# Second MLP's third combination made inside the convolution's output projection, with a hand-written order for the blocks around it

## The chip, the cores and the metric

The kernel runs on one core of one Trainium2 chip. A core has TensorE (PE, matrix products, with its weight loads shown as PEld), VectorE (DVE), ScalarE (ACT), GpSimd (POOL) and SyncE (SP, which here only issues DMAs). The metric is the device time of one execution in microseconds (us). The kernel before ran three times, with a median of 1697.54 us (1696.33 to 1698.54).

## What is computed

Two layers are applied to 768 tokens (a sequence of 512 and one of 256, lying side by side as T = 768 columns) of width 1024. Each layer is a token mixer, a squared-ReLU MLP and a gated embedding, each behind an RMS norm. The edit lies between the second layer's mixer and its MLP:

```python
def short_conv(h, w_in, conv_w, w_out):
    b_gate, c_gate, u = jnp.split(h @ w_in, 3, axis=-1)
    z = c_gate * u
    ...                                        # depthwise, width 3, per sequence
    return (b_gate * conv) @ w_out

h = rms_norm(x, norm_mix[i])
x = x + short_conv(h, conv_w_in[j], conv_w[j], conv_w_out[j])   # layer 1
h = rms_norm(x, norm_mlp[i])
x = x + jnp.square(jax.nn.relu(h @ mlp_w_up[i])) @ mlp_w_down[i]
gate = jax.nn.sigmoid(rms_norm(x, norm_ple[i]) @ ple_w_gate[i])
x = x + (p[i] @ ple_w_proj[i]) * gate
```

`w_out` is 1024 x 1024, `mlp_w_up` 1024 x 4096 and `mlp_w_down` 4096 x 1024, all in float32.

## The kernel before, in words

*Layout.* The residual x is held transposed, as eight blocks `x(m)` of 128 partitions by 768 columns; H = 384 is half of the columns. `PAIRED` is the order 0, 4, 1, 5, 2, 6, 3, 7 in which blocks are worked on, so that m and m + 4 follow each other.

*Float32 products.* Every operand is split into a high part, rounded to a matmul format by ACT, and a low part, the rest, subtracted by DVE (`split`, L82 to L84; `Weights7.high` and `low`, L434 and L445). A product is three matmuls per block: high by high, high by low, low by high.

*Two kinds of product.* A plain product runs over all eight blocks for both halves of the columns. The seven-product form (`product7`, L466) takes a pair of weight blocks and two halves of the input as a 2 x 2 matrix and needs seven products instead of eight; for it, weights are summed on DVE (`sums32`, `sums14`, L409 to L415) and inputs are *combined*: for each m below 4 one combination of x(m) and x(m+4). A combination is two copies with the norm's gain on ACT (`copied`, L326), four sums on DVE (`t13`, L345 and L346; `t42`, L350 and L351), two highs on ACT (L355) and two lows on DVE (L361). There are four of them, for blocks (0, 4), (1, 5), (2, 6) and (3, 7).

*The norm.* `norm.block(m, x(m))` writes the high and low parts of a block (`plain_block`, L304 to L310) and adds its square to an accumulator (L195, L196). When all eight are in, the accumulator is split (`acc_parts`: `ah` on ACT, `al` on DVE), a product with ones sums it over the partitions (`ss`, L235), and `rstd_steps` makes the factor rstd: `logs` (v on DVE at L252, then ln, exp and a square on ACT at L254 to L256, ahead of them `table`, which loads ACT's function table unless `ready` is set), `newton` (L260) and `result` (L267). The MLP's products run on blocks that aren't yet multiplied by rstd; it comes in with the squared ReLU (`rectified`, L938; `squared`, L941).

*Output projection.* `project_add` makes eight products `mm` (L129), adds each to x (L830) and calls `norm.block`. After the blocks with i = 1 and 3 it weaves in the combinations (0, 4) and (1, 5). At i = 4 it fetches the MLP's first weight chunk, at i = 6 and 7 it splits it ("direct" holds w11 and w12, "second" w21 and w22).

*The second MLP.* Chunks u = 0 and 1 are plain (`up_plain`, matmuls at L995), all others take the seven-product form (`up`; its first one, u = 2, has its products in the tiles a, b, c and d). Chunk u = 0 uses "direct" for its first 48 matmuls and "second" for its last 48. While it runs, `up_plain` makes `acc_parts`, the table load, the combination (2, 6), the second chunk's splits, the norm's steps and the combination (3, 7); the second chunk's "direct" part is `zhi` and `zlo`. While u = 1 runs, DVE and ACT make the activations of u = 0 and the sums and splits for u = 2. At u = 2, ACT copies the first product (`c`, L1054) before TensorE may add to its tile again.

*Order.* Inside `tc.manual_schedule(engines={ACT, PE, DVE})` these three engines take their instructions in the order of the program text; this holds for the whole MLP. Outside of it, and so in all of `project_add` before, a scheduler orders them. SP's fetches follow the program's order; the raw weights have three buffers (`wraw`), the split ones two each (`whi`, `wlo`), the plain chunk's "direct" part one (`zhi`, `zlo`).

Of the kernel before, what the change touches and what calls it, by code (L numbers as in the profile page):

```python
# [13 lines left out]
AF = mybir.ActivationFunctionType  # L14
ALU = mybir.AluOpType
# [3 lines left out]
P = 128  # L19
D = 1024  # L20
KB = D // P
# [16 lines left out]
H = T // 2  # L38
# [9 lines left out]
def trunk_kernel(ctx: ExitStack, tc: tile.TileContext, a: dict, out: bass.AP):  # L48
    nc = tc.nc
    act, dve, pe = nc.scalar, nc.vector, nc.tensor  # L50
# [65 lines left out]
    def both(name="mm", tag=None):  # L116

        return [t[:, :H] for t in fresh(name, 2, tag)]
# [4 lines left out]
    def group2(ps, terms, first=True, last=True):  # L123

        n = len(terms)
        for i, (wh, wl, xh, xl) in enumerate(terms):
            for j, (w, x) in enumerate(((wh, xh), (wh, xl), (wl, xh))):
                for t, o, e in pieces(ps):
                    pe.matmul(t, lhsT=w, rhs=x[:, o:e], start=first and i == 0 and j == 0, stop=last and i == n - 1 and j == 2)  # L129
# [22 lines left out]
    def big(name, dt=F32):  # L152

        nonlocal turn
        if more is None:
            return tmp.tile([P, T], dt, tag="t", name=name)
        turn += 1
        return tmp.tile([P, T], dt, tag=f"q{turn % 6}", name=name, bufs=1)

    def terms_of(w, xs, col=0):  # L160

        hi, lo = w
        c = slice(col, col + P)
        return [(wh[:, c], wl[:, c], xh, xl) for wh, wl, xh, xl in zip(hi, lo, *xs)]
# [6 lines left out]
    class Norm:  # L171
# [108 lines left out]
    class Norm7(Norm):  # L280
# [17 lines left out]
        def plain_block(self, m, xb):  # L298
            g = gain(self.i, m)
            if m < KB // 2:  # L300
                for j, t in enumerate((self.place(), slot(self.x12.pop(0), "x12"))):
                    src = xb[:, j * H : j * H + H]
                    hi, lo = t[:, :H], t[:, H:]
                    act.activation(hi, src, AF.Copy, scale=g)  # L304
                    dve.scalar_tensor_tensor(lo, src, g, hi.bitcast(F32), ALU.mult, ALU.subtract)
                    self.xs[("x11", "x12")[j]][m] = hi, lo
            else:
                hi, lo = self.place(), self.place()
                act.activation(hi[:], xb, AF.Copy, scale=g)
                dve.scalar_tensor_tensor(lo[:], xb, g, hi[:].bitcast(F32), ALU.mult, ALU.subtract)  # L310
                for j, k in enumerate(("x21", "x22")):
                    self.xs[k][m - KB // 2] = hi[:, j * H : j * H + H], lo[:, j * H : j * H + H]
# [158 lines left out]
    def mixer_attention():  # L471
# [346 lines left out]
    psum = ctx.enter_context(tc.tile_pool(name="ps", bufs=8, space=PSUM))  # L818
# [4 lines left out]
    def x(m, o=0, n=T):  # L823
        return pairs[m // 2][:, m % 2, o : o + n]

    def add(m, ps, src=None):

        src = x(m) if src is None else src
        for t, o, e in pieces(ps):
            dve.tensor_tensor(x(m)[:, o:e], src[:, o:e], t, ALU.add)  # L830


    PAIRED = [m + i for m in range(KB // 2) for i in (0, KB // 2)]

    def project_add(w, src, norm, behind, first):

        for i, m in enumerate(PAIRED):
            ps = both()
            ts = terms_of(first if i == 0 else weight(w[m], KB), src)
            group2(ps, [ts[k] for k in (*PAIRED[:6], *PAIRED[:5:-1])])  # L840
            add(m, ps)
            norm.block(m, x(m))
            behind(i)

    def up_chunk(l, u):
        f = 4 * (u // 2) + u % 2
        return Weights7(a["up"][l, f], a["up"][l, f + 2], plain=u < PLAIN[l])
# [4 lines left out]
    def weave(*chains):  # L852

        for steps in itertools.zip_longest(*chains):
            for step in steps:
                if step:
                    step()

    def first_chunk(l, norm, early):


        w = []

        def behind(i):
            if i == 4:
                w.append(up_chunk(l, 0))
            if i == 6:
                w[0].split("direct")
            if i == 7:
                w[0].split("second")  # L870
            if i % 2 and i // 2 < early:
                weave(norm.combine(i // 2))

        return w, behind

    ET = mybir.EngineType

    def second_inputs(places):

# [45 lines left out]
        weave(norm.combine(1))  # L925
        return parts

    def mlp(l, norm, nxt, w, places, early, product=None):


        xs = norm.xs
        r = parts = None
        todo = list(range(early, KB // 2))
        groups = [{k: {} for k in QS7.values()} for _ in range(NG)]
        pend = []
# [30 lines left out]
        def late(n=1):  # L966

            for _ in range(n):
                if pend:
                    pend.pop(0)()  # L970

        def up_plain(u, w, make, then):

# [14 lines left out]
            for n, (i, ks, sides) in enumerate(order):  # L988
                for k in range(*ks):
                    m, h = PAIRED[k] % (KB // 2), PAIRED[k] // (KB // 2)  # L990
                    c = slice(P * m, P * m + P)
# [172 lines left out]
                        nxt.block(m, x(m))  # L1164

        ups = [(up if u >= PLAIN[l] else up_plain, u) for u in range(2 * NG)]
        jobs = ups[:2]
        for g in range(NG - 1):
            jobs += [ups[2 * g + 2], (down, g, 0), (down, g, 1), ups[2 * g + 3]]
        with tc.manual_schedule(engines={ET.Activation, ET.PE, ET.DVE}):  # L1170
            if product:
                parts = ahead(norm, product, w, places[5:7] + places[12:])
                todo = todo[2:]
            for i, (job, *args) in enumerate(jobs):
# [12 lines left out]
                w = job(*args, w, make, lambda j: weight(a["down"][l, (NG - 1) * (KB // 2) + j], FG))  # L1187
# [117 lines left out]
    def last_ple(norm, full, rest, prs, ys, finals):  # L1305
# [64 lines left out]

        ET = mybir.EngineType
        with tc.manual_schedule(engines={ET.Activation, ET.PE, ET.DVE}):
# [41 lines left out]
        f = (KB, 2 * KB, 0)[kind] + p  # L1414
        return Weights7(a["w_in"][f], a["w_in"][f + KB // 2], plain)

    def mixer_conv(norm, w, v, norm_parts, held, finals, places, outs):
# [11 lines left out]
        pend, after, kept, done = [], [], {}, {}  # L1429
        ys = [None] * KB, [None] * KB  # L1430
# [160 lines left out]
        ET = mybir.EngineType  # L1591
        with tc.manual_schedule(engines={ET.Activation, ET.PE, ET.DVE}):
            for i, (kind, p) in enumerate(jobs):
# [12 lines left out]
        project_add(a["w_out"], ys, *outs, first=w)  # L1606

    class Last(Norm):
        def __init__(self, o, n, acc, rstd):
# [37 lines left out]
    n3 = Norm7(1, "mix1", xs3, aside3, rest[24], spare=dict(zip(("ah", "al", "v"), old[13:])))  # L1647
    wc = ple(n2, n3)

    n4 = Norm7(3, "mlp1", xs1, act1[7:11], act1[11])  # L1650
    w1, behind = first_chunk(1, n4, 2)
    mixer_conv(n3, *wc, held, finals[:], parts, (n4, behind))
    n5 = Norm(5, "ple1", xs1[:16], xs1[16])
    mlp(1, n4, n5, w1[0], act1, 2)
    last_ple(
        n5,
        full=xs1[17:] + act1[:1],
# [2 lines left out]
        ys=act1[8:11],  # L1660
        finals=((act1[11], act1[12]), (act1[13], xs1[16])),
# [79 lines left out]
```

## Time and profile before

| | |
|---|---|
| median of three runs | 1697.54 us |
| profiled execution | 1697.29 us |
| its span, first to last instruction | 1695.6 us |
| mean granted TensorE clock | 0.993 |
| PE busy | 1651.5 us (97%) |
| PEld busy | 1590.6 us (94%) |
| DVE busy | 1414.4 us (83%) |
| ACT busy | 907.3 us (54%) |
| DMA moved | 144.58 MB, mean 85 GB/s |

Times in the rows are microseconds from the start of the span. A row of the timeline has the start, the duration, the engine, the line of the kernel, the operation, the tile written and those read, the shape and the count, and in brackets how long the engine had been idle and what released it. Rows of the same kind that follow each other are merged; the end of a matmul is modelled, so one matmul's duration (0.34) is longer than its distance to the next (0.175). The granted clock is the share of full speed that TensorE was given.

### The profile page before, as it was taken

Reading aid. Unit: us, or ns where it says so; the run is one execution under the profiler, and the core shown is the slowest. Engines: PE = TensorE matmul, PEld = TensorE weight load, DVE = VectorE, ACT = ScalarE, POOL = GpSimd, SP = SyncE. Lnnn points to the kernel's source line nnn. Section 1 sums busy time; section 2 is a strip of 40 time slices with the busy share of each in tenths; the row PEclk is TensorE's granted clock in tenths of the full one; section 3 lists DMA queues with packets and bytes.
Section 4 is the critical chain, followed back from the end, with each engine's and each line's share of the span. In section 5 each row is a group of like instructions: output and inputs, shape, how many; then the busy total and the mean of one; then the engine's idle time right before and its main releaser. Section 6 shows DMA issues by size and latency. Waiting matters only on the chain.

```text
span 1695.6 us, 24086 instructions
## 1 busy us (share of the span) xinstructions
PE 1651.5 (97%) x9410; PEld 1590.6 (94%) x9410; DVE 1414.4 (83%) x2304; ACT 907.3 (54%) x1451; POOL 1.0 (0%) x12
## 2 busy tenths in 40 slices
PE   8999999989999999999999999999999999999996
PEld 7887788989999999999999999999999999999986
DVE  7588888889999989987888787858999999998776
ACT  6467756755455455544654334545445545554544
POOL 0000000000000000000000000000000000000000
PEclk9999999999999999999999999999999999999998
DMA  8653322212122212222312222211122222222222
GB/s 265 192 138 121 116 69 81 88 50 70 69 76 75 73 67 73 74 91 75 100 60 75 75 74 75 75 51 50 66 72 75 75 70 69 74 74 86 81 77 94
DMA packets 47842, 144.58 MB, mean 85 GB/s; under 512 B 6080, under 2 KB 10688, under 8 KB 47728
## 3 DMA queue, kind: packets, MB, share of 16 engines
q1 hardware_dynamic: 45168, 139.89, 25.0%
q10 hardware_dynamic: 2560, 3.15, 0.7%
q8 instruction: 74, 1.21, 0.3%
q14 instruction: 40, 0.33, 0.1%
HBM read 123.10 MB, written 10.48 MB: 79 GB/s over the span
## 4 chain that ended last, share of the span: by engine, by line
PE 59%; DVE 29%; ACT 8%; issue 3%; DMA 0%; DVEq 0%; ACTq 0%; SPq 0%
PE a L466 18%; PE mm L129 9%; PE mm L138 9%; PE b L466 4%; PE B L466 3%; PE C L466 3%; DVE t L361 3%; DVE wlo L445 3%; DVE y L938 3%; PE gate L138 3%; DVE zlo L445 2%; DVE act L394 1%; PE c L466 1%; ACT y L941 1%; PE d L466 1%
## 5 line engine op out<-in xcount | busy, mean ns | idle before, releaser
L434 ACT ACTIVATE whi<-sum 128x1024 fp32r<-128x1024 f32 x67 | 70.5, 1052 | 146.9 <-PE a L466 146.9
L941 ACT ACTIVATE y<-y 128x768 f32<-128x768 f32 x64 | 53.7, 840 | 144.6 <-DVE y L938 144.4
L466 PE MATMUL a<-xs,whi 128*128 128x384 f32 x624 | 122.2, 337 | 4.1 <-ACT whi L434 3.4
L466 PE MATMUL a<-t,zhi 128*128 128x384 f32 x536 | 111.3, 341 | 4.3 <-ACT c L1054 4.3
L466 PEld LDWEIGHTS a<-xs,whi 128*128 128x128 f32 x624 | 110.1, 188 | 4.8 <-ACT whi L434 3.7
L466 PE MATMUL b<-t,zhi 128*128 128x384 f32 x536 | 108.7, 336 | 0.0
L466 PE MATMUL a<-t,whi 128*128 128x384 f32 x536 | 108.7, 336 | 0.0
L466 PEld LDWEIGHTS a<-t,zhi 128*128 128x128 f32 x536 | 96.1, 190 | 5.2 <-ACT c L1054 5.0
L466 PE MATMUL a<-act,whi 128*128 128x384 f32 x448 | 96.5, 337 | 0.0
L466 PEld LDWEIGHTS a<-t,whi 128*128 128x128 f32 x536 | 94.8, 188 | 0.0
L466 PEld LDWEIGHTS b<-t,zhi 128*128 128x128 f32 x536 | 94.7, 188 | 0.0
L445 DVE TENSOR_TENSOR wlo<-wraw,whi 128x1024 fp32r<-128x1024 f32 x72 | 87.6, 1217 | 6.0 <-ACT whi L434 6.0
L445 DVE TENSOR_TENSOR wlo<-sum,whi 128x1024 fp32r<-128x1024 f32 x67 | 81.8, 1221 | 10.2 <-ACT whi L434 10.2
L1110 DVE TENSOR_TENSOR x<-x,a 128x384 f32<-128x384 f32 x112 | 60.7, 552 | 34.0 <-PE a L466 33.6
L434 ACT ACTIVATE zhi<-sum 128x1024 fp32r<-128x1024 f32 x67 | 71.0, 1060 | 22.7 <-DVE sum L410 22.7
L138 PE MATMUL mm<-xs_mix,whi 128*128 128x512 f32 (+1 forms) x320 | 82.8, 342 | 0.0
L434 ACT ACTIVATE whi<-wraw 128x1024 fp32r<-128x1024 f32 x72 | 75.7, 1052 | 11.5 <-PE C L466 6.0
L445 DVE TENSOR_TENSOR zlo<-sum,zhi 128x1024 fp32r<-128x1024 f32 x67 | 81.5, 1217 | 0.0
L466 PEld LDWEIGHTS a<-act,whi 128*128 128x128 f32 x448 | 79.9, 188 | 0.0
L355 ACT ACTIVATE t<-y 128x768 fp32r<-128x768 f32 x56 | 47.1, 841 | 39.8 <-DVE y L346 29.9
L83 ACT ACTIVATE whi<-wraw 128x1024 fp32r<-128x1024 f32 (+2 forms) x49 | 49.9, 1019 | 33.9 <-PE mm L129 14.0
L466 PE MATMUL a<-xs,wlo 128*128 128x384 f32 x312 | 67.2, 337 | 0.3 <-DVE wlo L445 0.2
(317 smaller groups left out, 4485.6 us busy)
## 6 DMA issues: line engine op xcount, KB each, us to landing
wraw<-in_up SPq DMA_DIRECT2D x64, 512.0 KB, 3.5
wraw<-in_down SPq DMA_DIRECT2D x64, 512.0 KB, 3.5
wraw<-in_w_in SPq DMA_DIRECT2D x24, 512.0 KB, 3.4
wraw<-in_gate SPq DMA_DIRECT2D x16, 512.0 KB, 3.4
pj<-pjs SPq DMA_DIRECT2D x16, 384.0 KB, 3.2
wraw<-in_w_q SPq DMA_DIRECT2D x8, 512.0 KB, 5.0
wraw<-in_w_out SPq DMA_DIRECT2D x8, 512.0 KB, 3.5
x_in<-in_x SPq DMA_DIRECT2D x8, 384.0 KB, 6.9
```

The source lines that it names most:

```text
L83: first = act.activation(hi, src, AF.Copy)
L129: pe.matmul(t, lhsT=w, rhs=x[:, o:e], start=first and i == 0 and j == 0, stop=last and i == n - 1 and j == 2)
L138: pe.matmul(ps[:, o:e], lhsT=w, rhs=x[:, o:e], start=i == 0 and j == 0, stop=i == n - 1 and j == 2,)
L355: act.activation(t[0][:], (self.q1, self.q2)[i][:], AF.Copy)
L361: dve.tensor_tensor(lo[:], (self.q1, self.q2)[i][:], hi[:].bitcast(F32), ALU.subtract)
L394: dve.tensor_tensor(lo[:], self.q2[:], hi[:].bitcast(F32), ALU.subtract)
L434: act.activation(hi[:], src, AF.Copy)
L445: dve.tensor_tensor(lo[:], src, hi[:].bitcast(F32), ALU.subtract)
L466: pe.matmul(ps, lhsT=a, rhs=b, start=start and i == 0, stop=i == len(terms) - 1, skip_group_check=True)
L938: dve.scalar_tensor_tensor(t[:, o:e], src, 0.0, r[:, o:e], op, ALU.mult)
L941: act.activation(t[:], t[:], AF.Square)
L1110: dve.tensor_tensor(t[:, o : o + H], t[:, o : o + H], f, op)
```

## The change

1. `project_add` no longer calls a `behind` function. Blocks i = 0 to 4 stay as they were, with the combinations (0, 4) and (1, 5). From the sixth product on (i = 5) a `manual_schedule` region orders ACT, PE and DVE as written: the split of the seventh weight block, block 5, the split of the eighth, the seventh product, the fetch of the first chunk, the copies and the first sums of the combination (2, 6), the eighth product, and then the splits of the first chunk between the parts of block 6 and of the combination; the rest of the combination, the copy of x(3), the fetch of the second chunk; then block 7, with the accumulator's split, the combination (3, 7) and the second chunk's "second" split.
2. The norm is marked `ready`, so its table load is left out.
3. `mlp` gets `begun`, the second chunk and the accumulator's parts. Its first chunk runs in the new `up_begun`, which has no combination: the first 48 plain matmuls, `ss`, `logs`, the second chunk's "direct" split, `newton`, `result`, then the last 48 matmuls and the squared ReLU. The number of combinations still to be made in the MLP is zero (`early` = 4).
4. `first_chunk` goes.

The diff, without the plain matmul loop, which is copied from `up_plain`:

```diff
-    def project_add(w, src, norm, behind, first):
-
-        for i, m in enumerate(PAIRED):
+    def project_add(w, src, norm, first):
+        def product(i, wt):
             ps = both()
-            ts = terms_of(first if i == 0 else weight(w[m], KB), src)
+            ts = terms_of(wt, src)
             group2(ps, [ts[k] for k in (*PAIRED[:6], *PAIRED[:5:-1])])
+            return ps
...
+        for i in range(5):
+            block(i, product(i, first if i == 0 else weights(i)))
+            if i in (1, 3):
+                weave(norm.combine(i // 2))
+        ps = product(5, weights(5))
+        norm.ready = True
+        with tc.manual_schedule(engines={ET.Activation, ET.PE, ET.DVE}):
+            w6 = weights(6)
+            block(5, ps)
+            w7 = weights(7)
+            ps = product(6, w6)
+            c = up_chunk(1, 0)
+            sums = norm.copied(2, 6)
+            sums.t13()
+            sums.t42()
+            ps7 = product(7, w7)
+            c.high("direct")
+            add(PAIRED[6], ps)
+            c.low("direct")
+            norm.plain_block(PAIRED[6], x(PAIRED[6]))
+            c.high("second")
+            norm.square(PAIRED[6], x(PAIRED[6]))
+            c.low("second")
+            sums.high(0)
+            sums.high(1)
+            norm.copied(3)
+            sums.low(0)
+            sums.low(1)
+            v = up_chunk(1, 1)
+            m = KB - 1
+            add(m, ps7)
+            norm.plain_block(m, x(m))
+            sq = big("sq")
+            act.activation(sq[:], x(m), AF.Square)
+            sums = norm.copied(m)
+            dve.tensor_tensor(norm.acc, norm.acc, sq[:], ALU.add)
+            parts = norm.acc_parts()
+            sums.t13()
+            sums.high(0)
+            v.split("second")
+            sums.t42()
+            sums.high(1)
+            sums.low(0)
+            sums.low(1)
+        return c, v, parts
...
+        def up_begun(u, w, make, then):
+            nonlocal r
+            v, parts = begun
+            ps = [both(f"p{i + 1}", "A") for i in range(2)]
+            plain_block(ps[0], 0, w)
+            ss = norm.sum_squares(psum, parts=parts, tag="C")
+            logs, newton, result = norm.rstd_steps(psum, ss)
+            logs()
+            v.split("direct")
+            newton()
+            result()
+            r = norm.r
+            y = [big(f"y{i + 1}") for i in range(2)]
+            for i in range(2):
+                if i:
+                    plain_block(ps[1], 1, w)
+                for o in range(2):
+                    rectified(y[i], ps[i][o], H * o, H * o + H, ALU.max)
+                if i == 0:
+                    squared(y[0])
+            pend.extend(acts_of(u, *y, y[1]))
+            return v
...
-    w1, behind = first_chunk(1, n4, 2)
-    mixer_conv(n3, *wc, held, finals[:], parts, (n4, behind))
+    w1, *begun = mixer_conv(n3, *wc, held, finals[:], parts, n4)
     n5 = Norm(5, "ple1", xs1[:16], xs1[16])
-    mlp(1, n4, n5, w1[0], act1, 2)
+    mlp(1, n4, n5, w1, act1, KB // 2, begun=begun)
```

More of the change, by code (lines that the diff above doesn't have):

```diff
@@ L830, in add, with weights, block @@
             dve.tensor_tensor(x(m)[:, o:e], src[:, o:e], t, ALU.add)
+    ET = mybir.EngineType
     PAIRED = [m + i for m in range(KB // 2) for i in (0, KB // 2)]
-    def project_add(w, src, norm, behind, first):
-        for i, m in enumerate(PAIRED):
+    def project_add(w, src, norm, first):
+        def product(i, wt):
             ps = both()
-            ts = terms_of(first if i == 0 else weight(w[m], KB), src)
+            ts = terms_of(wt, src)
             group2(ps, [ts[k] for k in (*PAIRED[:6], *PAIRED[:5:-1])])
+            return ps
+        def weights(i):
+            return weight(w[PAIRED[i]], KB)
+        def block(i, ps):
+            m = PAIRED[i]
             add(m, ps)
             norm.block(m, x(m))
-            behind(i)
+        for i in range(5):
[43 more added lines that the diff above has]
+        return c, v, parts
     def up_chunk(l, u):
@@ L857, in weave @@
                     step()
[L859 to L876, printed above, removed]
     def second_inputs(places):
@@ L926, in ahead, with mlp @@
         return parts
-    def mlp(l, norm, nxt, w, places, early, product=None):
+    def mlp(l, norm, nxt, w, places, early, product=None, begun=None):
         xs = norm.xs
@@ L970, in late, with plain_block @@
                     pend.pop(0)()
+        def plain_block(ps, i, w):
+            for k in range(KB):
+                m, h = PAIRED[k] % (KB // 2), PAIRED[k] // (KB // 2)
+                c = slice(P * m, P * m + P)
+                hi, lo = w.w[f"w{i + 1}{h + 1}"]
+                for j, (wt, part) in enumerate(((hi, 0), (hi, 1), (lo, 0))):
+                    for o in range(2):
+                        pe.matmul(
+                            ps[o],
+                            lhsT=wt[:, c],
+                            rhs=xs[f"x{h + 1}{1 + o}"][m][part],
+                            start=k == 0 and j == 0,
+                            stop=k == KB - 1 and j == 2,
+                        )
+        def up_begun(u, w, make, then):
[14 more added lines that the diff above has]
+                    plain_block(ps[1], 1, w)
+                for o in range(2):
+                    rectified(y[i], ps[i][o], H * o, H * o + H, ALU.max)
[3 more added lines that the diff above has]
+            return v
         def up_plain(u, w, make, then):
@@ L1166, in mlp @@
         ups = [(up if u >= PLAIN[l] else up_plain, u) for u in range(2 * NG)]
+        if begun:
+            ups[0] = (up_begun, 0)
         jobs = ups[:2]
@@ L1415, in conv_weights, with mixer_conv @@
         return Weights7(a["w_in"][f], a["w_in"][f + KB // 2], plain)
-    def mixer_conv(norm, w, v, norm_parts, held, finals, places, outs):
+    def mixer_conv(norm, w, v, norm_parts, held, finals, places, nxt):
         xs = norm.xs
@@ L1605, in mixer_conv @@
             split_out(KB // 2 - 1)
-        project_add(a["w_out"], ys, *outs, first=w)
+        return project_add(a["w_out"], ys, nxt, first=w)
     class Last(Norm):
```

## The prediction

> **What bounds the kernel now.** I read the first line of the page, then the busy time by stretches, then the timeline of each engine from 1054 to 1176 us, where the edited code runs. The first line shows TensorE busy for nearly the whole span:
>
> ```profile
> PE 1651.5 (97%) x9410; PEld 1590.6 (94%) x9410; DVE 1414.4 (83%) x2304; ACT 907.3 (54%) x1451; POOL 1.0 (0%) x12
> ```
>
> The stretches cut the edited part in three: the eight products of the output projection; the first two chunks of the second layer's MLP (u=0 and u=1, plain products); and the third chunk (u=2, the first one in the seven-product form).
>
> ```profile
> 1054.70:1122.20 67.50, 67.42 (x386) 66.53 (x385) 47.24 (x65) 32.37 (x41) 0.00 (x0) 1.00 0.22 78
> 1122.20:1156.30 34.10, 34.10 (x198) 34.09 (x197) 24.64 (x37) 20.78 (x26) 0.00 (x0) 1.00 0.09 32
> 1156.30:1176.20 19.90, 17.10 (x86) 16.14 (x85) 18.37 (x27) 9.86 (x14) 0.00 (x0) 0.91 0.16 53
> ```
>
> Columns: length of the stretch, then busy time of PE, PEld, DVE, ACT, POOL, then the granted clock. The reader sees that TensorE leaves no gap in the first two stretches (67.42 of 67.50 us, 34.10 of 34.10 us), while DVE and ACT have room there (47.24 and 32.37 us in the first). In the third, TensorE has 17.10 of 19.90 us, the granted clock falls to 0.91, and DVE is busy 18.37 us of 19.90. So work of DVE or ACT can shorten the run only through the third stretch. Its TensorE timeline, from the first row of u=2 to the first of the job behind it:
>
> ```profile
> 1156.35 1.56 PE L466 MATMUL a<-xs,whi 128*128 128x384 f32 x8
> ...
> 1160.92 0.97 PE L466 MATMUL b<-t,zlo 128*128 128x384 f32 x4 [0.51 <-DVE zlo L445]
> 1164.05 2.80 PE L466 MATMUL a<-t,zhi 128*128 128x384 f32 x8 [2.16 <-ACT c L1054]
> ...
> 1167.80 1.56 PE L466 MATMUL c<-xs,whi 128*128 128x384 f32 x8
> ...
> 1176.20 0.86 PE L466 MATMUL a<-act,whi 128*128 128x384 f32 x4
> ```
>
> u=2 takes 1176.20 - 1156.35 = 19.85 us. An undisturbed job of the same seven products is the last one of the convolution:
>
> ```profile
> 1040.05 1.56 PE L466 MATMUL a<-xs,whi 128*128 128x384 f32 x8
> ...
> 1054.72 0.86 PE L129 MATMUL mm<-ys,whi 128*128 128x384 f32 x4
> ```
>
> It takes 1054.72 - 1040.05 = 14.67 us, or 2.10 us a product. u=2 loses 19.85 - 14.67 = 5.18 us. Of this, 0.51 us is a wait for DVE's zlo and 2.16 us one for ACT's copy c; the product s2 at 1164.05 then takes 3.75 us to 1167.80 instead of 2.10, at a clock of 0.56:
>
> ```profile
> 1165.00:1168.00 3.00, 3.00 (x12) 3.00 (x12) 2.59 (x5) 1.80 (x5) 0.00 (x0) 0.56 0.00 0
> ```
>
> Those are 0.51 + 2.16 + 1.65 = 4.32 us; the remaining 0.86 are smaller slips around the first two products.
>
> Why are zlo and c late? DVE's timeline:
>
> ```profile
> 1127.08 0.96 DVE L84 TENSOR_TENSOR al<-acc_mlp,ah 128x768 fp32r<-128x768 f32 x1 [0.91 <-ACT ah L83]
> ...
> 1131.11 1.22 DVE L445 TENSOR_TENSOR wlo<-wraw,whi 128x1024 fp32r<-128x1024 f32 x1 [0.39 <-ACT whi L434]
> ...
> 1133.31 2.01 DVE L361 TENSOR_TENSOR t<-q,t 128x768 fp32r<-128x768 f32 x2
> 1135.32 1.23 DVE L445 TENSOR_TENSOR zlo<-wraw,zhi 128x1024 fp32r<-128x1024 f32 x1
> 1136.46 1.01 DVE L252 TENSOR_SCALAR v<-ss 128x384 f32<-128x384 f32 x2
> ...
> 1143.20 2.01 DVE L361 TENSOR_TENSOR t<-q,t 128x768 fp32r<-128x768 f32 x2
> 1145.13 0.95 DVE L260 SCALAR_TENSOR_TENSOR v<-ln,v 128x768 f32<-128x768 f32 x1
> ...
> 1147.11 1.95 DVE L938 SCALAR_TENSOR_TENSOR y<-p,rstd_mlp 128x384 f32<-128x384 f32 x4
> ...
> 1159.65 1.22 DVE L445 TENSOR_TENSOR zlo<-sum,zhi 128x1024 fp32r<-128x1024 f32 x1
> 1160.78 1.94 DVE L938 SCALAR_TENSOR_TENSOR y<-p,rstd_mlp 128x384 f32<-128x384 f32 x4
> ```
>
> and ACT's:
>
> ```profile
> 1127.07 1.28 ACT L216 ACT_TABLE_LOAD   x1
> ...
> 1130.98 0.83 ACT L355 ACTIVATE t<-q 128x768 fp32r<-128x768 f32 x1
> ...
> 1134.24 1.04 ACT L434 ACTIVATE zhi<-wraw 128x1024 fp32r<-128x1024 f32 x1
> 1137.04 1.05 ACT L254 ACTIVATE ln<-ss,eps 128x384 f32<-128x384 f32 x2 [1.76 <-DVE v L252]
> ...
> 1139.76 1.75 ACT L326 ACTIVATE q<-x,vec 128x768 f32<-128x768 f32 x2
> ...
> 1161.83 0.84 ACT L941 ACTIVATE y<-y 128x768 f32<-128x768 f32 x1 [4.73 <-DVE y L938]
> ...
> 1163.52 0.47 ACT L1054 ACTIVATE c<-a 128x384 f32<-128x384 f32 x1
> ```
>
> At 1147.11 DVE first multiplies by rstd_mlp (`rectified`, called the rects here). From there to zlo, the rects at 1160.78, ACT's square at 1161.83 and the copy c at 1163.52 it is one queue with almost no idle time. rstd itself was late: between v (1136.46) and newton (1145.13) stand the two copies q on ACT at 1139.76 and the sums of the fourth combination, ending with the lows at 1143.20.
>
> **The change part by part.** The sum is made against the profiled execution, 1697.29 us (span 1695.6 us and 1.7 us around it); the median of the three runs is 1697.54, 0.25 us above.
>
> *Third combination (blocks 2 and 6) into the projection.* Two copies (0.92 us each, half of the row at 1139.76 with its overlap), four DVE sums (0.56), two highs (0.83) and two lows (half of 2.01): about 3.5 us on ACT and 4.2 on DVE. They leave the time after TensorE's 1122.23 and lie beside products 6 and 7, where the first stretch leaves DVE 20 us and ACT 35 us. Cost on the path: nothing, as product 7 is issued ahead of them; without that cover they would be the up to 4.2 us that they cost now.
>
> *Order of the last blocks, ACT and DVE.* Block 5 stands ahead of the split of w7. That split is done by about 1110.7 (add from 1105.6, its block and the accumulator until 1109.5, wlo 1.2), and product 7 starts near 1113.9: hidden by 3 us. The first chunk's splits fall at 1111 to 1116 ("direct") and 1116 to 1120 ("second"); TensorE wants them from 1122.2 and 1131.3. Hidden.
>
> *SP.* The fetches stay the same 512 KB each, but in another order:
>
> ```profile
> 1070.79 4.29 SPq L89 DMA_DIRECT2D wraw<-in_up  x2
> 1078.75 12.69 SPq L89 DMA_DIRECT2D wraw<-in_w_out  x3
> ```
>
> The first chunk's two fetches, now at 1070.79, move behind the last three of w_out, to where buffers come free (the splits of w5 and w6, about 1091 and 1099), the second chunk's to about 1111 and 1116. With 3.5 us from issue to landing all are there 10 us or more before their split:
>
> ```profile
> wraw<-in_up SPq DMA_DIRECT2D x64, 512.0 KB, 3.5
> ```
>
> Nothing on the path; POOL has no part in it.
>
> *Last block and first chunk.* The order of TensorE's matmuls stays as it is up to u=1, so it should reach these times again:
>
> ```profile
> 1122.23 0.34 PE L995 MATMUL p<-xs,zhi 128*128 128x384 f32 x1
> ...
> 1130.60 0.34 PE L235 MATMUL ss<-ah,ones 128*128 128x384 f32 x1
> ...
> 1139.66 0.51 PE L995 MATMUL p<-x,zhi 128*128 128x384 f32 x2
> 1140.01 0.33 PE L995 MATMUL p<-x,zlo 128*128 128x384 f32 x1
> ```
>
> The table load of 1.28 us goes (the norm is marked ready); it stood ahead of the third combination's copies, so it counts only through the chain that follows. al ends at 1128.04 as before, and the *fourth* combination comes in the place of the third:
> - its first two sums to 1129.15, a high (0.83) to 1129.95, then ACT's "second" split of the next chunk to 1130.95 (1.04 as at 1134.24);
> - wlo of it from 1131.0 instead of 1131.11, then, as now, 2.20 us to the lows and 2.01 for them: v at about 1135.1, not 1136.46, since zlo of "direct" no longer stands ahead of it;
> - ln 0.58 after v (1137.04 - 1136.46): 1135.7; the three ACT steps take 1139.76 - 1137.04 = 2.72: 1138.4. Now comes zhi (1.04), on DVE zlo from 1139.45 to 1140.67, 1.14 to newton as from zlo to v now: 1140.6; the rects 1.98 behind newton (1147.11 - 1145.13): 1142.57.
>
> So rstd is used 1147.11 - 1142.57 = 4.5 us sooner. Gain in u=2: the queue from the rects to c is unchanged and takes 1163.52 - 1147.11 = 16.4 us at most, so c is possible from 1159.0, zlo ends at 1156.3, and wlo moves with them. TensorE, even if 0.8 us late, ends its first product of u=2 at 1159.25 and needs zlo at 1160.7 and the copied c at 1161.35. All of the 5.18 us goes; what is late next there is c, with 1.6 us to spare.
>
> *The new wait.* zlo of "direct" was written at 1135.32 and is now wanted while DVE is still at it: u=1 starts with zhi at 1139.66 and wants zlo at 1140.01; it ends at 1140.67. TensorE waits 0.7 to 0.9 us; I take 0.8. Behind zlo on DVE stand newton and rstd (counted above); for TensorE's wait everything behind it waits. From below, 0: if ln needn't wait for v, zhi is done 1 us sooner. But ACT waited for v each time:
>
> ```profile
>   DVE v L252: 10.9, 8
> ```
>
> From above, the nearest row is the start of the convolution, where the last block came late in such an order by hand:
>
> ```profile
> 879.81 0.61 PE L1517 MATMUL c<-xs,zhi 128*128 128x384 f32 x2 [0.94 <-ACT xs L309]
> 880.87 0.62 PE L1517 MATMUL c<-xs,zhi 128*128 128x384 f32 x2 [0.44 <-DVE xs L310]
> ...
> 879.00:882.00 3.00, 1.75 (x8) 1.43 (x9) 1.45 (x2) 2.54 (x3) 0.00 (x0) 1.00 0.02 5
> ```
>
> 0.94 + 0.44 = 1.38 us, at a clock of 1.00: so 0 to 1.4 us, without a fall of the clock.
>
> Sum: 1697.29 - 5.18 + 0.8 = 1692.9 us, or -0.26%; with the ends, 1692.1 to 1693.5.
>
> [...]
>
> **The rivals.** *The slow product stays.* If the low clock at 1165 to 1168 has another cause than the idle time ahead of it, only 5.18 - 1.65 goes: 1697.29 - 3.53 + 0.8 = 1694.6. For it: the two waits are short. Against: the clock is 1.00 in both stretches ahead.
>
> *The wait moves to u=1.* If DVE or ACT is 1.5 us later than worked out (the sums, the split and v are a chain of ten steps across two engines), zlo comes at 1142.2, the wait is about 2.3 us, as long as the 2.16 that cost 1.65 more in clock: 5.18 - 2.3 - 1.65 = 1.2 us are left, 1696.1. For it: the new chain has no slack at all. Against: most of its steps run now in the same order with the same releasers.
>
> *Slower.* The second chunk's "second" split needs a w buffer. There are two. If it got the one with the first chunk's "second" halves, which TensorE reads until 1139.66, ACT would stand at that split from 1129.95 to 1139.7, and with it the sums, v and zlo, 9.75 us later: zlo ends at 1150.4. Wait 10.5, clock 1.65, gain 5.18: 1697.29 + 7.0 = 1704.3. It decides once zlo ends after about 1143.5 (3.5 us of wait and 1.65 of clock use up the gain). Against: the same four splits take w buffers now, and wlo of this one runs at 1131.11, long before 1139.66.
>
> **How the numbers follow.** Forecast, all of u=2's loss gone and up to 1.4 us of new wait (1692.1 to 1693.5): 65%. The slow product stays (1694.6): 7%. The wait moves (1694 to 1697.2): 18%. Slower by more: 6%. The remaining 4% are a larger gain, from fewer DVE jobs in the chunk behind. 0.2% is 3.4 us, about what a measurement of this kernel can tell from no change, so faster means below 1694.15: the forecast, the larger gain and a few of the second case, 70%; within, 24%; slower, 6%. The range goes from the forecast's lower end less 1 us (the runs shown lie up to 1.2 us from their median) to the middle of the moved wait, 1691.0 to 1696.1.
>
> **What the profile after would show.** No table load at 1127; the copies and sums of blocks 2 and 6 before 1122 and TensorE without a gap up to there; v near 1135.1 and the first use of rstd near 1142.6; a wait of TensorE of 0.7 to 0.9 us for zlo at the start of u=1, clock 1.00; u=2 at 14.7 us with no wait for c; u=0 unchanged. Wrong if TensorE waits in the projection (a split late), if v comes after 1136.5, or if u=2 still shows a wait for c.

## The result, and the profile after

The changed kernel takes 1693.95 us (median of eight runs, 1692.19 to 1695.21), the kernel before, run beside it, 1699.01 us (eight runs, 1696.33 to 1701.46). The ratio is 0.997 with an interval of 0.9959 to 0.9981, so the change saves 3.2 to 7.0 us; the difference of the medians is 5.06 us. The profiled execution of the changed kernel took 1694.92 us, with a span of 1692.9 us at a mean granted clock of 0.993.

The busy line of the page hardly tells the two kernels apart: PE was at 1651.5 us and is at 1650.7, and ACT has one instruction fewer, the table load.

```profile
PE 1650.7 (98%) x9410; PEld 1591.0 (94%) x9410; DVE 1415.0 (84%) x2304; ACT 905.7 (54%) x1450; POOL 1.0 (0%) x12
```

The busy time by stretches does. These are the same three stretches, each shifted with the code (columns as in the prediction):

```profile
1056.90:1124.40 67.50, 67.40 (x386) 66.53 (x385) 51.39 (x71) 36.09 (x46) 0.00 (x0) 1.00 0.23 76
1124.40:1158.50 34.10, 34.10 (x198) 34.10 (x197) 25.94 (x38) 16.21 (x21) 0.00 (x0) 1.00 0.15 50
1158.50:1173.10 14.60, 14.60 (x85) 14.60 (x84) 12.43 (x19) 9.06 (x13) 0.00 (x0) 1.00 0.11 36
```

In the third one, u=2, TensorE now fills all 14.60 us at a clock of 1.00 (it had 17.10 of 19.90 us at 0.91). The work taken out of u=0 and u=1 shows in ACT's column (16.21 us there, 20.78 before) and turns up in the projection (36.09, before 32.37), where TensorE still has no gap. TensorE's timeline of u=2, with the job behind it as the last row:

```profile
1158.47 1.56 PE L466 MATMUL a<-xs,whi 128*128 128x384 f32 x8
...
1161.96 0.86 PE L466 MATMUL b<-t,zlo 128*128 128x384 f32 x4
1162.66 1.55 PE L466 MATMUL a<-t,zhi 128*128 128x384 f32 x8
...
1164.76 1.55 PE L466 MATMUL c<-xs,whi 128*128 128x384 f32 x8
...
1173.14 0.86 PE L466 MATMUL a<-act,whi 128*128 128x384 f32 x4
```

No row of u=2 has a bracket, so TensorE waited for nothing. The job takes 1173.14 - 1158.47 = 14.67 us, exactly the undisturbed job of the convolution, and the product s2 takes 1164.76 - 1162.66 = 2.10 us where it took 3.75. The copy c, which TensorE had waited for, now waits for TensorE (ACT's timeline):

```profile
1160.77 0.47 ACT L1130 ACTIVATE c<-a 128x384 f32<-128x384 f32 x1 [0.56 <-PE a L466]
```

**The balance.** From the projection's first matmul to the first one behind u=2 it was 1176.20 - 1054.72 = 121.48 us; now it is 1173.14 - 1056.86 = 116.28, that is 5.20 less. The span fell by only 2.7 us because this execution came 2.14 us later to the projection, and lost 0.36 us behind it. The order of the instructions of every engine is the same in both kernels up to the projection, so the 2.14 us are no work of the change. 0.63 us of them are there by 158 us; 1.47 us more come from one place in layer 0's attention. First its windows and two rows of TensorE's timeline in the kernel before:

```profile
156.00:160.00 4.00, 2.34 (x13) 1.82 (x14) 3.95 (x10) 2.62 (x6) 0.00 (x0) 1.00 0.95 275
160.00:164.00 4.00, 2.28 (x14) 1.76 (x12) 2.04 (x5) 3.42 (x13) 0.00 (x0) 1.00 0.94 273
```

```profile
158.10 0.70 PE L726 MATMUL pt<-ident,L 128*128 128x128 f32 x4 [0.68 <-DVE L L721]
...
164.14 0.73 PE L138 MATMUL mm<-p,whi 128*128 128x512 f32 x2 [1.86 <-ACT pjs L521]
```

and the same in the changed kernel:

```profile
156.00:160.00 4.00, 2.33 (x10) 1.66 (x10) 3.96 (x15) 2.41 (x5) 0.00 (x0) 0.83 1.02 318
160.00:164.00 4.00, 4.00 (x20) 3.42 (x18) 1.76 (x3) 2.64 (x9) 0.00 (x0) 0.74 1.00 252
```

```profile
158.73 1.11 PE L726 MATMUL pt<-ident,L 128*128 128x128 f32 x4 [0.68 <-DVE L L721]
...
166.24 0.73 PE L138 MATMUL mm<-p,whi 128*128 128x512 f32 x2 [1.85 <-ACT pjs L521]
```

The waits are alike (0.68 us ahead of the first row in both, 1.86 and 1.85 us ahead of the second), but the granted clock fell to a mean of 0.83 and 0.74 in one execution (it was 0.50 from 158.64 to 162.06) and stayed at 1.00 in the other. The second row comes 166.24 - 158.73 = 7.51 us behind the first in the changed kernel and 164.14 - 158.10 = 6.04 us in the other: these are the 1.47 us, and the clock is the one thing in the rows that differs. So two single profiled executions differ by some 2 us, nearly half of what the edit is worth, at places that it does not touch. The stretch around the edit (-5.20) and the medians of eight runs (-5.06) agree; the spans (-2.7) are the wrong pair to compare.

### The profile page after: what moved, and what is told of

The parts are those of the page before. It is cut to its first block, busy times and chain, and to the rows that moved or that the text cites. A ratio compares the mean times of both kernels' runs of the same rounds, so it can differ in the third digit from the quotient of the medians.

```text
span 1692.9 us, 24085 instructions
## 1 busy us (share of the span) xinstructions
PE 1650.7 (98%) x9410; PEld 1591.0 (94%) x9410; DVE 1415.0 (84%) x2304; ACT 905.7 (54%) x1450; POOL 1.0 (0%) x12
## 4 chain that ended last, share of the span: by engine, by line
PE 60%; DVE 29%; ACT 7%; issue 3%; DMA 0%; DVEq 0%; ACTq 0%; SPq 0%
PE a L466 17%; PE mm L129 9%; PE mm L138 9%; PE b L466 4%; PE gate L138 4%; PE B L466 3%; PE C L466 3%; DVE t L361 3%; DVE wlo L445 3%; DVE y L974 3%; DVE zlo L445 2%; DVE act L394 1%; DVE sum L410 1%; ACT y L977 1%; DVE sum L409 1%
## 5 line engine op out<-in xcount | busy, mean ns | idle before, releaser
L445 DVE TENSOR_TENSOR vlo<-wraw,vhi 128x512 fp32r<-128x512 f32 x67 | 46.1, 689 | 24.8 <-ACT vhi L434 24.8
```

The lines of the kernel that those rows point to most:

```text
L445: dve.tensor_tensor(lo[:], src, hi[:].bitcast(F32), ALU.subtract)
```

## The experiments

The theory: u=2 lost its 5.2 us because rstd was late, and moving the third combination out of the way of rstd removes that. Open were whether the dropped table load or the hand-written order did it instead, why the new wait at u=1 did not come, and what the slow product hung on. In each experiment below "the stretch" is the time from the projection's first matmul to the first one behind u=2 (121.48 us before, 116.28 after), and "the rects" is the start of the first multiplication by rstd, counted from the start of u=0 (24.88 before, 19.31 after). Several kernels shared the runs of the kernel before, whose median was 1700.1 us beside the table load put back, the late copy and the two of layer 0, and 1699.06 us beside the other four. The medians tell a gain of 5 us from none; differences of 1 to 2 us lie within their intervals and are read from the stretch, that is from one profiled execution of each kernel.

### The third combination back in u=0

```diff
-            sums = norm.copied(2, 6)
-            sums.t13()
-            sums.t42()
...
-            sums.high(0)
-            ...
-            norm.copied(3)
-            sums.low(0)
-            ...
+            norm.copied(2)
...
-            sums = norm.copied(m)
+            sums = norm.copied(6)
...
             v.split("direct")
+            weave(norm.combine(3))
             newton()
```

All else stays as in the changed kernel: the hand-written order, no table load.

> The changed kernel with the combination of blocks 2 and 6 taken out of the projection; it is made in the place of the one of blocks 3 and 7, and that one again between logs and newton in the first chunk. No table load, the hand order and the new first chunk stay. If moving the combination is what brings rstd sooner, the first use of rstd goes from 19.3 us behind the start of u=0 (1143.69 - 1124.38) to about 24 (4.4 us of DVE work and part of the copies), u=2 from 14.67 to 18 to 20 us, and the stretch from the projection's first matmul to the first one behind u=2 from 116.28 to 120 to 121.5 us. The rival, that the missing table load and the order of the splits do it, leaves u=2 at 14.7 and the stretch at 116.3.

It took 1698.68 us, ratio 0.9995 (0.9986 to 1.0005). The stretch is 120.17 us, u=2 takes 18.56 us, and the rects start at 23.58. TensorE waits for c again, and the clock is low behind it (timeline of TensorE, then a window):

```profile
1165.70 1.77 PE L466 MATMUL a<-t,zhi 128*128 128x384 f32 x8 [2.07 <-ACT c L1124]
```

```profile
1167.10:1170.51 3.41, 3.41 (x13) 3.41 (x12) 3.20 (x6) 2.68 (x5) 0.00 (x0) 0.50 0.01 2
```

So without the move most of the loss is there, 18.56 - 14.67 = 3.89 of 5.18 us. What is left as a gain, 121.48 - 120.17 = 1.3 us, is the share of everything else in the change together.

### The kernel before without the table load

```diff
+    n4.ready = True
     w1, behind = first_chunk(1, n4, 2)
```

> The kernel before with the norm marked ready, so that only its table load of 1.28 us goes. If the moved combination is the cause, rstd comes 1.3 us sooner (23.6 us behind the start of u=0 instead of 24.9) and u=2 falls from 19.85 to 17 to 18.6 us, depending on whether the clock still falls; the stretch is 118.6 to 120.2 us. If the table load was the cause, u=2 is near 14.7 and the stretch near 116.3.

It took 1698.26 us, ratio 0.9993 (0.9983 to 1.0003), with a stretch of 120.10 us, u=2 at 18.45 us and the rects at 23.47.

```profile
1162.43 2.21 PE L466 MATMUL a<-t,zhi 128*128 128x384 f32 x8 [1.96 <-ACT c L1054]
```

The wait for c went from 2.16 to 1.96 us and the wait for zlo is gone. The load's 1.28 us head the chain in the kernel before and rstd comes 1.4 us sooner without it, yet u=2 stays late: 1.4 us gained, about as much as the previous experiment had left (1.3). Both runs' intervals include 1, so that these 1.3 to 1.4 us are seen in the stretch alone.

### The table load put back into the changed kernel

```diff
-        norm.ready = True
         with tc.manual_schedule(engines={ET.Activation, ET.PE, ET.DVE}):
```

> The changed kernel with the table load back (the norm isn't marked ready). If the moved combination is worth what its return cost (120.17 - 116.28 = 3.9 us) whatever the table load does, u=2 stays at 14.7 us. The load, 1.28 us ahead of ln, makes zlo end 18.7 us behind u=0's start instead of 17.4, so TensorE waits 0.7 to 1.0 us at the start of u=1: the stretch is 117.1 to 117.4 us. If the two gains only add up, 3.9 and 1.4, u=2 keeps a wait and the stretch is 117.7.

It took 1694.28 us, ratio 0.9966 (0.9953 to 0.9979), with a stretch of 116.28 us, the same as without the load. The expected wait did not come. ACT's timeline says why:

```profile
1130.81 1.28 ACT L216 ACT_TABLE_LOAD   x1
1132.96 0.85 ACT L355 ACTIVATE t<-q 128x768 fp32r<-128x768 f32 x1 [0.87 <-DVE q L346]
```

In the new order the load falls behind ah, where ACT has nothing to do until DVE's sums are in: the high at 1132.96 waits for q even so, 0.87 us after the load has ended. The same instruction that cost 1.4 us ahead of the copies costs nothing here. So the whole 5.2 us come without dropping the load. (The hand-written order is still there in this run; the next one takes it away, without the load. No run has the move with neither.) The load's 1.4 and the move's 5.2 do not add up, because after the move u=2 has nothing left to lose.

### The projection's tail without the hand-written order

```diff
-        with tc.manual_schedule(engines={ET.Activation, ET.PE, ET.DVE}):
+        with nullcontext():
```

> The changed kernel without the order by hand in the projection; the moved combination, the missing table load and the new first chunk stay. If only the moved work counts, there is no wait of TensorE from the projection to u=2 and the stretch is 116.3 us. If the order by hand is needed, TensorE waits in the projection or at the start of u=0 or u=1, 1 us or more, and the stretch is 117.3 or more.

It took 1694.65 us, ratio 0.9967 (0.9957 to 0.9977), with a stretch of 116.27 us. TensorE has no wait in the projection, at u=1 or in u=2. Here the scheduler has the last sums and lows of the fourth combination done by 1134.27, and DVE then waits 0.59 us for `ss`:

```profile
1134.86 1.02 DVE L252 TENSOR_SCALAR v<-ss 128x384 f32<-128x384 f32 x2 [0.59 <-PE ss L235]
```

So v starts as soon as ss is there, and the rects start even sooner, at 16.46. The order by hand is not needed for the gain.

### One region from the projection's tail to the MLP

```diff
-        with tc.manual_schedule(engines={ET.Activation, ET.PE, ET.DVE}):
+        def tail(ps=ps):
...
-        return c, v, parts
+            return c, v, parts
+        return tail
...
         with tc.manual_schedule(engines={ET.Activation, ET.PE, ET.DVE}):
+            if begun:
+                w, *begun = begun()
```

The `with` line at the end is the one in `mlp`. The text and its order stay the same, but both parts stand in one ordered region instead of two that follow each other.

> The changed kernel with the projection's last blocks inside the MLP's ordered region, so that DVE takes the two v instructions behind the lows of the last combination, as the text has them. By the prediction's chain v starts 12.9 us behind u=0's start, zlo ends at 18.4, and TensorE waits 0.7 to 0.9 us for it at the start of u=1: a stretch of 117.1 us. The rival, that the place of v doesn't matter, leaves zlo at 17.4, no wait and 116.3.

It took 1694.98 us, ratio 0.9978 (0.9968 to 0.9987), with a stretch of 117.31 us. u=2 takes 14.67 us, but u=0 and u=1 together take 35.12 us instead of 34.09. TensorE's row at the start of u=1, then DVE's and ACT's rows ahead of it:

```profile
1141.48 0.45 PE L1074 MATMUL p<-x,zlo 128*128 128x384 f32 x1 [0.64 <-DVE zlo L445]
```

```profile
1133.84 2.01 DVE L361 TENSOR_TENSOR t<-q,t 128x768 fp32r<-128x768 f32 x2
1135.77 1.02 DVE L252 TENSOR_SCALAR v<-ss 128x384 f32<-128x384 f32 x2
1140.21 1.22 DVE L445 TENSOR_TENSOR zlo<-wraw,zhi 128x1024 fp32r<-128x1024 f32 x1 [3.42 <-ACT zhi L434]
```

```profile
1136.41 1.05 ACT L254 ACTIVATE ln<-ss,eps 128x384 f32<-128x384 f32 x2 [1.55 <-DVE v L252]
```

v stands behind both lows, as the text has it, ln waits 1.55 us for v, and zlo comes too late for TensorE by 0.64 us (1.03 us in all). This is the chain that the prediction worked out; the changed kernel as built does not run it. The 1.03 us are seen in the stretch; the interval of the run times overlaps that of the changed kernel.

### The copy c made late again

```diff
             c = bank("A" if first else "C", "c")[:, :H]
+            if first and l == 1:
+                for _ in range(8):
+                    junk = more.tile([P, 512], F32, tag="junk", name="junk", bufs=1)
+                    act.activation(junk[:], ones32[:, None, :].broadcast_to([P, 4, P]), AF.Copy)
             act.activation(c, a, AF.Copy)
```

> The changed kernel with eight extra copies of 128x512 on ACT (about 0.52 us each) ahead of the copy c in the second layer's u=2; they write a tile that nothing reads. ACT has 0.56 us idle there and c 1.4 us to spare, so TensorE should wait about 2.2 us for c, as in the kernel before. If an idle time of 2 us costs clock whenever it comes, the product s2 behind it takes 3.7 us instead of 2.10 and u=2 18.5 us. If the fall of the clock depends on where in its own period the wait comes, s2 takes anything from 2.1 to 3.8 and u=2 16.9 to 18.5 us.

Its one run took 1699.72 us; what it shows is in the trace. The stretch is 120.98 us and u=2 takes 19.36 us. TensorE's timeline and a window behind the wait:

```profile
1165.80 2.93 PE L466 MATMUL a<-t,zhi 128*128 128x384 f32 x8 [2.98 <-ACT c L1134]
...
1169.44 1.55 PE L466 MATMUL c<-xs,whi 128*128 128x384 f32 x8
```

```profile
1165.57:1168.98 3.41, 3.18 (x10) 3.18 (x11) 1.85 (x3) 2.97 (x6) 0.00 (x0) 0.50 0.00 0
```

The wait came out at 2.98 us, longer than the 2.2 us aimed at. s2 takes 1169.44 - 1165.80 = 3.64 us at a clock of 0.50, and the job loses 19.36 - 14.67 = 4.69 us, 1.71 more than the wait. The low clock comes back with the wait and, as the changed kernel shows, leaves with it.

### The same idea in layer 0

```diff
                     steps = [] if known else norm.rstd_steps(psum, ss)
+                    s = None
+                    if steps and product:
+                        m = todo.pop(0)
+                        s = norm.copied(m, m + KB // 2)
                     for step in steps[:1]:
                         step()
+                    if s:
+                        s.t13()
+                        s.t42()
+                        for step in steps[1:]:
+                            step()
...
+                        s.high(0)
+                        s.high(1)
+                        s.low(0)
+                        s.low(1)
```

The first of `steps` is `logs`, the others are `newton` and `result`. In the changed kernel layer 0's MLP still makes its last combination between the logs and newton. From the start of its u=0 to the first matmul behind its u=2 it takes 371.98 - 314.71 = 57.27 us, where the undisturbed times of layer 1 are 34.09 + 14.67 = 48.76: 8.5 us are lost. (The expectation below names 20.92 us for this u=2; that was read to the job's last product, and the 8.5 us here is the full loss.) The second version also sets `n1.ready = True`, which drops the table load there.

> The changed kernel with one more edit in the first layer's MLP: the last combination's copies go ahead of logs, its four DVE sums into the time in which DVE waits for ln, and its highs and lows behind result. The first layer has the same loss at its own u=2 (20.92 us instead of 14.67). If a late rstd causes it there too, rstd's first use comes 3.0 to 3.4 us sooner and the stretch from u=0's start to the first matmul behind u=2 shrinks by about as much: 0.9950 of the kernel before in all. If something else holds the first layer's u=2 (its whi wait of 3.4 us), the stretch stays and the ratio is that of the change, 0.997.

> As layer0, and the first layer's norm marked ready too, so that its table load of 1.28 us goes (ACT has that table since the start of the attention). If the chain of DVE and ACT from the last block to u=2 sets the first layer's wait, everything in it comes another 1.2 us sooner: the stretch shrinks by 4.2 to 4.8 us and the ratio to the kernel before is 0.9943. If the load lies beside other work, the stretch is that of layer0.

The first took 1690.19 us, ratio 0.9941 (0.9929 to 0.9954), the second 1689.19 us, ratio 0.993 (0.9917 to 0.9943); both intervals lie below the changed kernel's (0.9959 to 0.9981), and they overlap each other. Both are a little faster than expected (0.9950 and 0.9943). The 57.27 us become 54.16 and 52.27, the rects start at 25.06 and 23.63 instead of 28.62. TensorE at the start of layer 0's u=2 and at its copy c, in the changed kernel, in the first version and in the second, and for the second the two windows across which its wait for c lies:

```profile
352.42 2.32 PE L466 MATMUL a<-xs,whi 128*128 128x384 f32 x8 [3.40 <-ACT whi L434]
...
360.27 1.67 PE L466 MATMUL a<-t,zhi 128*128 128x384 f32 x8 [1.82 <-ACT c L1130]
```

```profile
347.12 1.66 PE L466 MATMUL a<-xs,whi 128*128 128x384 f32 x8
...
354.96 2.51 PE L466 MATMUL a<-t,zhi 128*128 128x384 f32 x8 [2.16 <-ACT c L1144]
```

```profile
354.64 1.67 PE L466 MATMUL a<-t,zhi 128*128 128x384 f32 x8 [2.09 <-ACT c L1144]
...
364.15 1.65 PE L466 MATMUL a<-xs,whi 128*128 128x384 f32 x8 [0.86 <-DVE y L1167]
```

```profile
350.21:353.62 3.41, 2.35 (x14) 2.02 (x12) 3.11 (x6) 1.20 (x2) 0.00 (x0) 1.00 0.31 125
353.62:357.03 3.41, 2.39 (x14) 2.39 (x15) 2.28 (x3) 3.41 (x7) 0.00 (x0) 1.00 0.02 5
```

The wait of 3.40 us for whi is gone in the first version, the one for c is not: 2.09 us are still there in the second, and 0.86 us for y. The combination was only moved within u=0 here, not out of it, and a part comes back: 3.1 of 8.5 us in the first version, 5.0 in the second. Most of the 1.9 us between the two need not be the table load's: the execution of the changed kernel has 3.41 us at a clock of 0.50 in this u=2 (353.20 to 356.62), which cost up to 1.7 us (half of 3.41, an estimate), and for the 20 matmuls behind its wait for c the first version takes 360.12 - 354.96 = 5.16 us, where the second takes 358.24 - 354.64 = 3.60.

## Why the prediction was right, and where it was not

The prediction was right in its sign, its place and its cause. It forecast 1692.9 us from an execution of 1697.29, a saving of 4.4 us; the medians differ by 5.06 and the stretch by 5.20. The measured time is 1.05 us above the forecast, and two errors partly cancel in that: over eight runs the kernel before has a median of 1699.01 us, 1.72 above the execution that the sum was made against, and the saving is 0.7 us larger than forecast. That the time came out so close is in part luck; it lies just above the narrow forecast of 1692.1 to 1693.5, while the saving is that of its lower end.

**The loss in u=2.** All of 5.18 us was to go, and u=2 went from 19.85 to 14.67 us. With the combination put back (18.56 us) the loss returns, with the load put back or the hand-written order taken away (14.67) it does not. The cause named, a late rstd through the third combination, is shown. Across the runs u=2 follows the rects almost one for one: with the rects at 23.47, 23.58 and 24.88 us it takes 18.45, 18.56 and 19.85 us, and with the rects at 20.51, 19.31 or 16.46 it takes 14.67. The table load was a second cause of the late rstd, 1.4 us of the 5.2; the prediction let it count only through the chain and gave it no term of its own.

**The slow product.** It was counted as a part of the waits' price. s2 ran at 1.00 once the waits were gone, and at 0.50 once a wait of 2.98 us was put back. So the first rival, under which 1.65 us would have stayed, did not happen. In u=2 waits of 1.96 to 2.98 us had the low clock behind them (behind the one of 1.96 us, without the table load, the clock has a mean of 0.66 from 1164 to 1168 us). A wait does not have it each time: the 0.68 us in the attention rows above came with it in one execution and without it in the other, and so did the waits of 3.40 and 3.42 us in the last section.

**The cover in the projection.** 67.40 us of 67.50 are busy. SP's fetches of the first chunk moved behind w_out as worked out (forecast about 1091):

```profile
1093.26 8.66 SPq L89 DMA_DIRECT2D wraw<-in_up  x2
```

They are the two fetches of the first chunk, now at 1093.26 instead of 1070.79 (1091.1 with the 2.14 us taken off that this execution was late), and nothing on TensorE waits for their splits.

**The step that failed: the new wait, 0.8 us too many.** It was put at 0.7 to 0.9 us, with a lower end of 0 "if ln needn't wait for v". The 0 came, but not in that way: in none of the ten traces does a half of ln start before its half of v is done. It came because v itself was earlier than the sum had it. TensorE at the start of u=1, and DVE from al to the rects in the changed kernel:

```profile
1141.78 0.52 PE L1071 MATMUL p<-x,zhi 128*128 128x384 f32 x2
1142.14 0.33 PE L1071 MATMUL p<-x,zlo 128*128 128x384 f32 x1
```

```profile
1129.23 0.96 DVE L84 TENSOR_TENSOR al<-acc_mlp,ah 128x768 fp32r<-128x768 f32 x1 [0.91 <-ACT ah L83]
...
1133.19 1.23 DVE L445 TENSOR_TENSOR wlo<-wraw,whi 128x1024 fp32r<-128x1024 f32 x1 [1.94 <-ACT whi L434]
1134.33 0.55 DVE L350 SCALAR_TENSOR_TENSOR q<-q 128x384 f32<-128x384 f32 x1
1134.80 0.55 DVE L252 TENSOR_SCALAR v<-ss 128x384 f32<-128x384 f32 x1
1135.27 0.55 DVE L351 SCALAR_TENSOR_TENSOR q<-q 128x384 f32<-128x384 f32 x1
1135.73 0.95 DVE L361 TENSOR_TENSOR t<-q,t 128x768 fp32r<-128x768 f32 x1
1136.60 0.55 DVE L252 TENSOR_SCALAR v<-ss 128x384 f32<-128x384 f32 x1
1137.07 0.95 DVE L361 TENSOR_TENSOR t<-q,t 128x768 fp32r<-128x768 f32 x1
1140.57 1.23 DVE L445 TENSOR_TENSOR zlo<-wraw,zhi 128x1024 fp32r<-128x1024 f32 x1 [2.55 <-ACT zhi L434]
1141.71 0.95 DVE L260 SCALAR_TENSOR_TENSOR v<-ln,v 128x768 f32<-128x768 f32 x1
...
1143.69 1.95 DVE L974 SCALAR_TENSOR_TENSOR y<-p,rstd_mlp 128x384 f32<-128x384 f32 x4
```

The two halves of v stand between the sums and the lows of the fourth combination, ahead of where the text has them. The combination's last steps and v belong to two ordered regions, and where one follows the other the built order may mix them; the prediction took the text for the order across that seam. ACT's rows for it:

```profile
1136.78 1.05 ACT L254 ACTIVATE ln<-ss,eps 128x384 f32<-128x384 f32 x2
...
1139.49 1.04 ACT L434 ACTIVATE zhi<-wraw 128x1024 fp32r<-128x1024 f32 x1
```

ln has no bracket: it follows ACT's last high at once. It starts 1136.78 - 1124.38 = 12.40 us behind the start of u=0, 1.2 us sooner than where v stands behind the lows (1136.41 - 1122.82 = 13.59). So zlo ends at 1141.80, 17.42 us behind the start of u=0 instead of the forecast 18.44, just ahead of the matmul at 1142.14 that reads it. With the seam removed, zlo ended at 18.61, the rects started at 20.51 (forecast 20.34) and the wait was 0.64 us, 1.03 us in all: the sum of steps was sound, the order under it was not. The same shift makes rstd 5.6 us sooner instead of 4.5, which brings nothing more, since u=2 was already whole.

**The other rivals.** The moved wait, as an end near 1696.1 us, did not happen; the single region shows its mild form (0.64 us of waiting, 1.03 us in all). The slower case through the w buffer did not: ACT made the "second" split ahead of wlo at 1133.19, without waiting for TensorE's last use of the other one at 1141.

## What to carry to other kernels

Where the bounding engine is busy 97% of the time, look for the stretch in which it is not, and follow its waits back to a value that is late; here one norm factor, and the work that could leave its chain went under eight products with 20 us of room. Removing two things from one chain need not be worth the sum of both: each had its own gain (5.2 and 1.4 us), together they gave 5.2, as the chain then had slack. When a wait is worth less than a microsecond, take the order from the queues as built and not from the text, above all where two ordered parts meet.

## What the hardware showed that was not expected

Up to about half of what a short wait cost here is the clock behind it, and that part came in one length. Up to 50 us before the end of each trace, the granted clock fell three times in the kernel before (at 211.90, 358.67 and 1164.22 us) and three times in the changed kernel (at 158.64, 213.26 and 353.20 us), each time to 0.50 and for 3.41 us. From the end of one such time to the next fall it was 143.36 and 802.13 us in the kernel before, 51.20 and 136.53 us in the changed one: 42, 235, 15 and 40 times 3.413. A low time that TensorE works through loses half of it, 1.71 us (an estimate from the 0.50 and the 3.41 us). This fits u=2 of layer 1: waits for c of 1.96, 2.07 and 2.98 us cost 18.45 - 14.67 - 1.96 = 1.82, 1.82 and 1.71 us more than themselves.

Two waits of one length differ in it. In layer 0 TensorE waits for whi 3.42 us in the kernel before and 3.40 us in the changed kernel. Windows of 3.41 us, counted from the next fall in the same trace (358.67 and 353.20), first those in which the wait of the kernel before lies, then the one with most of the changed kernel's wait and the one behind it:

```profile
345.02:348.43 3.41, 1.77 (x11) 1.45 (x9) 3.19 (x6) 0.98 (x3) 0.00 (x0) 1.00 0.00 0
348.43:351.85 3.42, 1.63 (x8) 1.34 (x8) 3.38 (x5) 2.69 (x3) 0.00 (x0) 1.00 0.00 0
```

```profile
349.79:353.20 3.41, 0.78 (x4) 0.78 (x5) 3.34 (x7) 3.06 (x4) 0.00 (x0) 1.00 0.00 0
353.20:356.62 3.42, 3.42 (x13) 3.38 (x12) 3.42 (x4) 0.12 (x1) 0.00 (x0) 0.50 0.38 111
```

The first wait lies in both of its windows, so that TensorE works 1.77 and 1.63 us in them, and the clock stays at 1.00. The second leaves 0.78 us of work in one window, and the next runs at 0.50. The wait of 2.09 us in layer 0 left 2.35 and 2.39 us of work in its two windows, at a clock of 1.00 in both. In the 3.41 us ahead of the six falls TensorE worked 1.92, 1.25 and 1.14 us in the kernel before and 1.83, 2.25 and 0.78 us in the changed one. Other windows counted in the same way had no fall behind them, with 1.58 us of work (160.70 to 164.11) and 2.03 us (877.50 to 880.91) in the kernel before. What decides between them, the runs do not show. No run moved a wait with all else the same, so this is a reading of two traces and not a test.

A function table load of 1.28 us cost 1.4 us where it heads the chain to rstd, and nothing where ACT would have idled.
